# The second latent expert layer and the attention projections in plain float32, with half of that layer's gates carried by VectorE's one-hot operand

## The chip, the cores and the metric

One core of a Trainium2 chip runs the whole program in one launch. The metric is the device time of that launch in microseconds (us). Engines are named as in the profile: PE (TensorE matmul), PEld (its weight loads), DVE (VectorE), ACT (ScalarE), POOL (GpSimd), SP (SyncE, which issues most loads).

## The reference, cut to what matters

The model is a two-layer block with sparse attention, followed by a second block: per layer a mixer (gated delta rule in layer 0, grouped-query attention in layer 1) and an expert layer `peer` with 16384 experts. Only layer 1 of the second block is touched. All tensors are float32; there are 256 latent tokens of width 1024.

```python
def attention_mixer(h_ctx, h_lat, w_in, qn_g, kn_g, w_out, cos, sin, need_ctx_out):
    p = h @ w_in                  # 256 x 1024 by 1024 x 1536: q (8 heads), k and v (2 heads) of 128
    q_l = apply_rope(rmsnorm(q_l, qn_g), cos, sin); k_l = apply_rope(rmsnorm(k_l, kn_g), cos, sin)
    o_l = gqa_attend(q_l, concat(k_c, k_l), concat(v_c, v_l))     # softmax attention
    return o_l.reshape(B, T, ATT_Q_W) @ w_out                     # 256 x 1024 by 1024 x 1024
...
def peer(h, w_query, sub_keys, u_tab, v_tab):                     # per token x
    qry = (xb @ w_query).reshape(P, PEER_HEADS, 2, PEER_HALF)
    s = jnp.einsum('phcd,hckd->phck', qry, sub_keys)
    top_s, top_i = lax.top_k(s, PEER_TOPK)                        # 16 of 128, twice per head
    ...
    best_s, pos = lax.top_k(cand_s, PEER_TOPK)                    # 16 of the 256 pairs
    gate = jax.nn.softmax(best_s, axis=-1)
    act = jax.nn.gelu(jnp.einsum('pd,phkd->phk', xb, u_tab[idx]), approximate=False)
    return jnp.einsum('phk,phkd->pd', gate * act, v_tab[idx])
```

## The kernel before, in words

**The expert layer.** For the latent tokens `lat_peer` evaluates all 16384 experts densely: 128 chunks of 128 experts. `Dense.up` (L1876) multiplies one chunk's u-rows, two tiles `ut` of 128x512, with the normalised hidden state and puts gelu of it into the table G. `Dense.spread` (L1914) makes the gates of four tokens at a time: `L` holds a one-hot row of the second expert index times the gate (ACT: Abs, then Relu, L1923 and L1925), `R` a one-hot row of the first (DVE, L1926), and four matmuls `gp` multiply them. The gates are multiplied into G (L1938 where gelu is there already; else ACT copies them, L1940, and `up` multiplies later, L1910). `Dense.down` (L1956) multiplies G with the v-rows, one tile `vt` of 128x512 for each chunk and half of the output columns, 256 tiles in all.

**Layer 1 of it** keeps the first 48 tokens out of the dense work (`nb = 48`, so T = 208 columns): the class `Few` fetches their 16 experts per head by indirect DMA from POOL, 48 gathers for u-rows (`fg`, L1799, dotted on DVE at L1813) and 48 for v-rows (`gv`, L1737, summed on DVE at L1742). Each gather moves 128 rows of 4 KB; two buffers hold them (GB = 2).

**Precision.** A product is either plain float32 or *split*. `split` (L503) has ACT copy a weight tile rounded to fp32r (`sh`, L511) and DVE subtract (`sl`, L513); the activations are split once (`xs`). The product then is sh times [hi, lo], 416 or 512 columns, plus sl times hi. In layer 1 with `nb` the two halves land side by side in the bank and are added afterwards: in `up` by an ACT copy (L1902) and a DVE add (L1903). In `up` half of the contraction is split (four of eight steps), in `down` three of four chunks (`FD = 4`), there with a split of G as well (`gs`, L1976 and L1977). In the attention all of both projections is split (`lin_rows_split`, L537). In traces a plain float32 product appears as two MATMUL records, a split one as one record for each operand.

**Order.** A scheduler places the instructions; it runs on a model of its own. `weave(M.prep, ups, *WP)` mixes the routing (`peer_route`: 16 query projections `acs`, then top-k on DVE) with the first N0 = 56 chunks of `up`. `up_spread` then makes one spread for each of 52 chunks and does the last 20 alone. `down` follows, output half 0 then 1. Gathers are paced: `tick` adds its microseconds times a rate (FRATE = 0.1), and at each whole step one gather is traced under `issue_after(E.pin)`, where `E.pin` is the last instruction that was pinned (`split`'s subtraction, L513). They start at chunk 48 (`FAT`).

**Buffers.** Weight tiles come from one pool of five (UB = 5) tiles of 256 KB; a tile is free for its next load when its last reader is done: a split tile after ACT and DVE have read it, a plain tile after its last matmul. The banks `y` in PSUM (four) serve `up` and then `down`; `cf` has two buffers.

```python
UB, HB, VB, OB, N0, GB = 5, 5, 5, 2, 56, 2
DPS = dict(acc=1, ps=1, gp=2, y=4)
NB, FRATE, FAT, LAST = (0, 48), 0.1, 48, 48
```

Of the kernel before, what the change touches and what calls it, by code (L numbers as in the profile page):

```python
# [516 lines left out]
def split_x(E, P, hT, name, xs=None, nb=0):  # L517

    nc = E.nc
# [3 lines left out]
    for k in range(n):  # L523
        hi = xs[:, k, 0:256]
        if k % 2:
            nc.vector.tensor_copy(hi, hT[:, k])
# [3 lines left out]
        for lo, t in ((256, slice(nb, 256)), (512 - nb, slice(0, nb))):  # L530
            if t.stop > t.start:
                eng.tensor_tensor(out=xs[:, k, lo:lo + t.stop - t.start], in0=hT[:, k, t], in1=hi[:, t].bitcast(F32),
                                  op=ALU.subtract)
    return xs


def lin_rows_split(E, P, xs, w, width, fn):  # L537

    p = [acc(E) for _ in range(2)]
    for k in range(len(w)):  # L540
        h, l = split(E, P, w[k], k)
        for tt in range(2):
            for q, (o, wp) in enumerate(((0, h), (0, l), (256, h))):
                mm(E, p[tt][:, :width], xs[:, k, o + tt * 128:o + tt * 128 + 128], wp[:, :width], k == 0 and q == 0,
                   k == len(w) - 1 and q == 2)
    for tt in range(2):
        fn(tt, p[tt][:, :width])
# [9 lines left out]
def lin_cols_split(E, P, xs, ap, off, nt, fn, tag="acc", nb=0, xf=None):  # L557
# [4 lines left out]
    k0 = 4 if xf is not None else 0  # L562
    for t in range(nt):
        p = bank(E, tag, "acs")
        ws = wtile(E, ap, off + t * D * 128, 2, 512)
        for o in range(k0, 8, 4):
            h, l = split(E, P, ws[o // 4], o // 4)
            for k in range(4):
                c = slice(k * 128, k * 128 + 128)
# [1 line left out]
                end = o + k == 7 and not k0
                if nb:
                    mm(E, p, h[:, c], x, o + k == k0, False)
                    mm(E, p[:, 0:256], l[:, c], x[:, 0:256], False, end)
                else:
                    mm3(E, p[:, 0:256], h[:, c], l[:, c], x[:, 0:256], x[:, 256:512], o + k == k0, end)
# [3 lines left out]
        if nb:  # L580
            s = P.tile([128, 256], F32, name="ssum", tag="s", bufs=2)
            nc.scalar.copy(s[:, nb:256], p[:, 256:512 - nb])
            nc.scalar.copy(s[:, 0:nb], p[:, 512 - nb:512])
            nc.vector.tensor_tensor(out=s, in0=p[:, 0:256], in1=s, op=ALU.add)
            fn(t, s)
        else:
            fn(t, p[:, 0:256])
# [1252 lines left out]
class Dense:  # L1840
# [35 lines left out]
    def up(self, c, PU, n):  # L1876
# [10 lines left out]
        h, l = split(E, PU, us[0], 0)  # L1887
        for k in range(4):
            e = slice(k * 128, k * 128 + 128)
            x = self.xs[:, k, self.nb:self.nb + o1]  # L1890
            if self.nb:
                mm(E, p[:, 0:o1], h[:, e], x, k == 0, False)
                mm(E, p[:, 0:T], l[:, e], x[:, 0:T], False, False)
            else:
                mm3(E, p[:, 0:T], h[:, e], l[:, e], x[:, 0:T], x[:, T:o1], k == 0, False)
# [518 lines left out]
```

## Time and profile before

| what | value |
|---|---|
| runs (three) | 4258.22, 4268.22, 4280.0 us; median 4268.22 |
| profiled execution | 4277.75 us, span 4276.0 us, mean granted clock 0.942 |
| layer 1 of the second block in the span | attention from about 3225 us, routing from 3372, chunks from 3430, `down` from 3889 to 4264 us |
| PE, DVE, ACT, POOL busy in the whole span | 89%, 64%, 42%, 23% |

The profile is of one execution; times in it are counted from the start of its span. Matmuls overlap and their ends are modelled, so what one costs is read from the distance between starts in a dense stretch. The rest of the program, about 3225 us, is the same in both kernels.

### The profile page before, as it was taken

The page shows a single profiled execution, that of the slowest core. Times are in us where ns is not written, and L with a number is a line of the kernel's source. Part 1 is how long each engine was busy: PE and PEld are TensorE (multiplying, and loading weights), DVE is VectorE, ACT ScalarE, POOL GpSimd, SP SyncE. Part 2 cuts the span into 40 slices and gives each one's busy share as a digit, 9 for nine tenths or more (in the row PEclk, how much of TensorE's full clock was granted, in tenths as well). Part 3 has the DMA queues.
Part 4 walks back from the last instruction along what each step waited for, and adds up shares of the span by engine and source line. Part 5 has one row for each costly group of instructions (what it writes and reads, how often), then busy time and mean ns, then how long its engine had stood idle before and what let it go on. Part 6 is the DMA issues. An engine that isn't in the chain of part 4 may idle for free.

```text
span 4276.0 us, 66249 instructions
## 1 busy us (share of the span) xinstructions
PE 3790.3 (89%) x23253; PEld 3016.9 (71%) x23253; DVE 2721.5 (64%) x6361; ACT 1805.1 (42%) x4811; POOL 999.2 (23%) x973
## 2 busy tenths in 40 slices
PE   8787888979998799787789999999987899889998
PEld 6654565548555486674458899987866788888897
DVE  4683268568555684667328667766666696777764
ACT  3223212534225343422223379744434345984443
POOL 1010015453344532101002211112223122112110
PEclk8888998989998899898899999999999999999999
DMA  5443536899987996336334676688773256668875
GB/s 182 121 155 105 177 129 211 270 326 357 330 308 248 325 356 244 120 113 197 137 116 141 211 232 214 204 260 261 244 239 121 71 168 201 218 205 275 276 257 165
DMA packets 383518, 907.27 MB, mean 212 GB/s; under 512 B 87361, under 2 KB 89377, under 8 KB 382417
## 3 DMA queue, kind: packets, MB, share of 16 engines
q1 hardware_dynamic: 270080, 553.04, 39.0%
q0 software_dynamic: 87552, 318.81, 22.1%
q10 hardware_dynamic: 25552, 31.19, 2.4%
q8 instruction: 184, 3.01, 0.3%
q14 instruction: 150, 1.22, 0.1%
HBM read 887.56 MB, written 15.32 MB: 211 GB/s over the span
## 4 chain that ended last, share of the span: by engine, by line
PE 34%; DMA 15%; DVE 11%; ACT 5%; issue 4%; POOL 2%; SPq 0%; ACTq 0%; DVEq 0%; POOLq 0%
PE acc L392 8%; PE au L392 8%; PE y L392 7%; DMA vt<-in_peer_v_dram 7%; DMA ut<-in_peer_ut_dram 4%; PE acs L392 4%; DVE sl L513 3%; ACT sh L511 2%; PE gp L392 2%; DMA gv<-in_peer_v_dram,ixz 1%; DMA w<-in_ada_w_dram 1%; DMA w<-in_peer_wq_dram 1%; POOL cand L1659 1%; PE S L392 1%; PE o L392 1%
## 5 line engine op out<-in xcount | busy, mean ns | idle before, releaser
L392 PE MATMUL y<-gs,sh 128*128 128x512 f32 (+1 forms) x1536 | 540.8, 406 | 48.5 <-DVE gs L1977 43.9
L392 PE MATMUL au<-hp,ut 128*128 128x256 f32 (+1 forms) x2048 | 456.6, 366 | 0.3 <-issue 0.2
L513 DVE TENSOR_TENSOR sl<-vt,sh 128x512 fp32r<-128x512 f32 x384 | 268.2, 703 | 236.1 <-ACT sh L511 215.4
L392 PE MATMUL acc<-hdn,w 128*128 128x256 f32 x1536 | 378.4, 401 | 39.6 <-issue 17.0
L511 ACT CAST sh<-vt 128x512 fp32r<-128x512 f32 x384 | 236.8, 619 | 415.6 <-DMA vt<-in_peer_v_dram 359.2
L392 PE MATMUL y<-gs,sl 128*128 128x256 f32 (+1 forms) x1536 | 403.0, 273 | 5.0 <-DVE sl L513 4.9
L392 PE MATMUL au<-xs,sh 128*128 128x256 f32 (+1 forms) x1536 | 390.8, 334 | 18.0 <-DVE cf L1903 16.5
L392 PEld LDWEIGHTS au<-hp,ut 128*128 128x128 f32 x2048 | 365.7, 194 | 21.8 <-DMA ut<-in_peer_ut_dram 0.8
L1724 DVE SCALAR_TENSOR_TENSOR gu<-gu,h 128x1024 f32<-128x1024 f32 x256 | 311.6, 1223 | 90.4 <-DMA gu<-in_peer_u_dram,ixs 81.8
L392 PEld LDWEIGHTS acc<-hdn,w 128*128 128x128 f32 x1536 | 298.4, 200 | 97.0 <-issue 26.2
L392 PEld LDWEIGHTS y<-gs,sh 128*128 128x128 f32 x1536 | 292.2, 192 | 100.9 <-DVE gs L1977 61.1
L1722 POOL DMA_INDIRECT gu<-in_peer_u_dram,ixs x256 | 270.6, 1057 | 357.2 <-DVE gu L1724 223.6
L392 PE MATMUL au<-xs,sl 128*128 128x256 f32 (+1 forms) x1024 | 287.0, 280 | 22.3 <-DVE sl L513 21.8
L392 PEld LDWEIGHTS y<-gs,sl 128*128 128x128 f32 x1536 | 291.0, 193 | 14.8 <-DVE sl L513 9.2
L513 DVE TENSOR_TENSOR sl<-ut,sh 128x512 fp32r<-128x512 f32 x256 | 180.2, 705 | 168.9 <-ACT sh L511 161.6
L392 PEld LDWEIGHTS au<-xs,sh 128*128 128x128 f32 x1536 | 263.6, 193 | 30.3 <-DVE cf L1903 20.8
L1737 POOL DMA_INDIRECT gv<-in_peer_v_dram,ixz x128 | 138.5, 1082 | 613.7 <-DVE y L1742 573.2
L511 ACT CAST sh<-ut 128x512 fp32r<-128x512 f32 x256 | 159.9, 625 | 247.5 <-DMA ut<-in_peer_ut_dram 234.5
L392 PE MATMUL y<-G,vt 128*128 128x256 f32 (+1 forms) x1024 | 224.9, 362 | 0.0
L392 PEld LDWEIGHTS au<-xs,sl 128*128 128x128 f32 x1024 | 199.1, 194 | 28.0 <-DVE sl L513 27.7
L392 PE MATMUL acs<-xs,sh 128*128 128x256 f32 (+1 forms) x896 | 203.7, 318 | 8.7 <-ACT sh L511 4.9
L1925 ACT ACTIVATE ohl<-ohl,sl 128x128 f32<-128x128 f32 x464 | 207.3, 506 | 0.0
(637 smaller groups left out, 8009.6 us busy)
## 6 DMA issues: line engine op xcount, KB each, us to landing
ut<-in_peer_ut_dram SPq DMA_DIRECT2D x512, 256.0 KB
vt<-in_peer_v_dram SPq DMA_DIRECT2D x512, 256.0 KB
w<-in_ada_w_dram SPq DMA_DIRECT2D x96, 512.0 KB
w<-in_dn_w_in_dram SPq DMA_DIRECT2D x96, 512.0 KB
w<-in_w_up_dram SPq DMA_DIRECT2D x88, 512.0 KB
wd<-in_w_down_dram SPq DMA_DIRECT2D x44, 512.0 KB
w<-in_w_in_dram SPq DMA_DIRECT2D x40, 512.0 KB
w<-in_dn_w_out_dram SPq DMA_DIRECT2D x32, 512.0 KB
```

The costliest lines, as they stand in the source:

```text
L392: return E.nc.tensor.matmul(out, lhsT=lhsT, rhs=rhs, start=start, stop=stop)
L511: nc.scalar.copy(h, src)
L513: E.pin = eng.tensor_tensor(out=l, in0=src, in1=h.bitcast(F32), op=ALU.subtract).ins
L1659: nc.gpsimd.tensor_tensor(out=eq[:, h], in0=eq[:, h], in1=fi[:, h, None, :].to_broadcast([128, 16, 16]), op=ALU.mult)
L1722: nc.gpsimd.indirect_dma_start(out=g, out_offset=None, in_=E.a["peer_u"], in_offset=bass.IndirectOffsetOnAxis(ap=ix[:, s, k:k + 1], axis=0))
L1724: nc.vector.scalar_tensor_tensor(out=g, in0=g, scalar=1.0, in1=h, op0=ALU.mult, op1=ALU.mult, accum_out=c[:, k:k + 1])
L1737: nc.gpsimd.indirect_dma_start(out=g, out_offset=None, in_=E.a["peer_v"], in_offset=bass.IndirectOffsetOnAxis(ap=ix[:, k:k + 1], axis=0))
L1925: nc.scalar.activation(L[:, j], L[:, j], AF.Relu, scale=col(3, j), bias=col(2, j))
```

## The change

In layer 1 of the expert layer (`self.plain`, set where `xs` is None, which is where `nb` is not 0) every product is plain float32: `split_x`, all `split` calls, the `cf` sum, `gs` and the `ssum` of the query projections go. In `spread` two of the four tokens keep their gate in `L`; for the other two `L` is a bare one-hot (one Relu over both with constants) and the gate is multiplied into `R` by two DVE operations. `E.pin` is now set in `spread`, so after the last spread nothing new is pinned. The attention's projections use `lin_rows` on the plain hidden state. Layer 0 keeps its form.

```diff
@@ lin_cols_split
-    k0 = 4 if xf is not None else 0
+    k0 = 8 if xs is None else 4 if xf is not None else 0
...
         for k in range(k0):
-            mm(E, p[:, 0:256], ws[0][:, k * 128:k * 128 + 128], xf[:, k], False, k == k0 - 1)
+            w = ws[k // 4][:, k % 4 * 128:k % 4 * 128 + 128]
+            mm(E, p[:, 0:256], w, xf[:, k], k0 == 8 and k == 0, k == k0 - 1)
...
@@ Dense.up
+        if self.plain:
+            for k in range(4):
+                mm(E, p[:, 0:T], us[0][:, k * 128:k * 128 + 128], self.xf[:, 4 + k, nb:256], k == 0, False)
+        else:
...
-        if self.nb:
-            nc.scalar.copy(cf, p[:, T:o1])
-            nc.vector.tensor_tensor(out=cf, in0=p[:, 0:T], in1=cf, op=ALU.add)
...
-            nc.scalar.activation(cf[:, 0:n], y[:, 0:n], AF.Gelu)
+            cf = PU.tile([128, T], F32, name="cf", tag="cf", bufs=2)
+            nc.scalar.activation(cf[:, 0:n], p[:, 0:n], AF.Gelu)
@@ Dense.spread
-        for j in range(4):
+        a = 2 if self.plain else 4
+        for j in range(a):
             nc.scalar.activation(L[:, j], L[:, j], AF.Relu, scale=col(3, j), bias=col(2, j))
...
+        if a < 4:
+            nc.scalar.activation(L[:, a:4], L[:, a:4], AF.Relu, bias=1.0, scale=-1.0)
+        i = nc.vector.tensor_tensor(out=R[:, 0:a], in0=self.iota[:, None, :].to_broadcast([128, a, 128]),
+                                    in1=self.sl[:, 0, t:t + a, None].to_broadcast([128, a, 128]), op=ALU.is_equal).ins
+        if self.plain:
+            E.pin = i
+        for j in range(a, 4):
+            nc.vector.tensor_scalar(R[:, j], self.iota, col(0, j), col(2, j), op0=ALU.is_equal, op1=ALU.mult)
@@ Dense.down
-            if c % FD == FD - 1:
+            if self.plain or c % FD == FD - 1:
                 for k in range(4):
-                    mm(E, self.y[k][:, 0:T], vt[:, k * 128:k * 128 + 128], g, False, end)
+                    mm(E, self.y[k][:, 0:T], vt[:, k * 128:k * 128 + 128], g, first and c == cs[0], end)
                 continue
@@ attention
-            split_x(E, P, hT, "xs", xs)
...
-            lin_rows_split(E, PU, xs, w, 512, lambda tt, q: p.append(q))
+            lin_rows(E, hT, w, 512, lambda tt, q: p.append(q))
...
-            nc.scalar.copy(os[:, h, 0:256], o)
-            nc.vector.tensor_tensor(out=os[:, h, 256:512], in0=o, in1=os[:, h, 0:256].bitcast(F32), op=ALU.subtract)
+            evac(E, os[:, h], o)
...
-            lin_rows_split(E, PU, os, w, 512, fo)
+            lin_rows(E, os, w, 512, fo)
```

**Where the order moves.** PE near the end of `down`'s output half 0 in layer 1 (one order row of a plain product stands for one matmul call; `G1_29303` is the second half of the table G, `y_...` are the four banks, `yT` the turn of the finished sums). Before, the end of a group of four chunks, three split and one plain:

```order
L392 MATMUL y_33271<-gs_35179,sh_35182 128x416
L392 MATMUL y_33271<-gs_35179,sl_35183 128x208
L392 MATMUL y_33272<-gs_35179,sh_35182 128x416
L392 MATMUL y_33272<-gs_35179,sl_35183 128x208
L392 MATMUL y_33269<-G1_29303,vt_35194 128x208
L392 MATMUL y_33270<-G1_29303,vt_35194 128x208
L392 MATMUL y_33271<-G1_29303,vt_35194 128x208
L392 MATMUL y_33272<-G1_29303,vt_35194 128x208
L1999 MATMUL yT_35210<-cst0_58,ys_35200 128x128
```

Of the change, from the last spread through the last 21 chunks of `up` and the whole of half 0 (`G_27450` and `G_28473` are the two halves of G):

```order
L392 MATMUL gp<-ohr,ohl 128x128 x4
L392 MATMUL au<-hp,ut 128x208 x168
L392 MATMUL y<-G_27450,vt 128x208 x256
L392 MATMUL y<-G_28473,vt 128x208 x256
L1978 MATMUL yT<-cst_58,ys 128x128 x2
```

PE's operands in `up`'s tail and in `down` are now the loaded tiles and G themselves; no row between them reads what ACT or DVE made of a weight tile.

DVE in the last 20 chunks of `up`, after the last spread (the first row is that spread's own). `sl` is the low part of a weight tile, `cf` the gelu of a chunk, `fg` a gathered row block. Before:

```order
L1938 TENSOR_TENSOR G1_29303<-gp_32676,G1_29303 128x4x43
L513 TENSOR_TENSOR sl_32884<-ut_32879,sh_32883 128x512
L1910 TENSOR_TENSOR G1_29303<-G1_29303,cf_32705 128x208
L1910 TENSOR_TENSOR G1_29303<-G1_29303,cf_32734 128x208
L1903 TENSOR_TENSOR cf_32760<-au_32739,cf_32760 128x208
L1903 TENSOR_TENSOR cf_32789<-au_32765,cf_32789 128x208
L1910 TENSOR_TENSOR G1_29303<-G1_29303,cf_32760 128x208
L1910 TENSOR_TENSOR G1_29303<-G1_29303,cf_32789 128x208
L1903 TENSOR_TENSOR cf_32815<-au_32794,cf_32815 128x208
L1903 TENSOR_TENSOR cf_32844<-au_32820,cf_32844 128x208
L513 TENSOR_TENSOR sl_32910<-ut_32905,sh_32909 128x512
L1813 SCALAR_TENSOR_TENSOR fg_32925,fc_27859<-fg_32925,fh_32510 128x1024
```

Of the change, in the middle of the same 20 chunks (`fc` holds the dots of the gathered rows, `gv` is a block of gathered v-rows, `fy0_31447` the first of the three sums of them):

```order
L1879 TENSOR_TENSOR G1_28473<-G1_28473,cf_31137 128x208
L1786 SCALAR_TENSOR_TENSOR fg_31391,fc_27441<-fg_31391,fh_30854 128x1024
L1879 TENSOR_TENSOR G1_28473<-G1_28473,cf_31156 128x208
L1786 SCALAR_TENSOR_TENSOR fg_31418,fc_27441<-fg_31418,fh_30854 128x1024
L1790 TENSOR_TENSOR fc_27441<-fc_27441,fg_27440 128x48
L1879 TENSOR_TENSOR G1_28473<-G1_28473,cf_31172 128x208
L1713 TENSOR_SCALAR fy0_31447<-gv_31448,fc_27441 128x1024
L1879 TENSOR_TENSOR G1_28473<-G1_28473,cf_31191 128x208
L1715 SCALAR_TENSOR_TENSOR fy0_31447<-gv_31475,fc_27441,fy0_31447 128x1024
L1879 TENSOR_TENSOR G1_28473<-G1_28473,cf_31207 128x208
L1715 SCALAR_TENSOR_TENSOR fy0_31447<-gv_31502,fc_27441,fy0_31447 128x1024
```

The operations on gathers moved forward: between the multiplication of chunk 107 (the first of 208 columns, there are 21) and that of chunk 125 stand 18 of them, one for nearly every chunk; before, one stood for about every two and a half chunks, and the rest lay in `down`.

## Rows read from the trace of the kernel before

**Rows 1.** The page of the kernel before: PE's busy time, share and instructions, and the chain that ended last by engine.

```profile
PE 3790.3 (89%) x23253; PEld 3016.9 (71%) x23253; DVE 2721.5 (64%) x6361; ACT 1805.1 (42%) x4811; POOL 999.2 (23%) x973
PE 34%; DMA 15%; DVE 11%; ACT 5%; issue 4%; POOL 2%; SPq 0%; ACTq 0%; DVEq 0%; POOLq 0%
```

**Rows 2.** Busy time by stage: window, its length, then busy us (and instructions) of PE, PEld, DVE, ACT and POOL, granted clock, DMA share, GB/s. In order: attention and norm; query projections; 108 chunks with 52 spreads; a dense part of these; the last 20 chunks; `down` in two stretches; and 235 us of layer 0's spreads.

```profile
3225.00:3372.00 147.00, 114.76 (x523) 90.90 (x521) 105.94 (x196) 57.57 (x149) 53.08 (x46) 0.91 0.28 95
3372.00:3430.00 58.00, 56.52 (x303) 48.77 (x304) 37.79 (x172) 18.92 (x56) 3.20 (x5) 1.00 0.45 141
3430.00:3842.00 412.00, 371.85 (x2233) 355.60 (x2231) 305.45 (x807) 294.63 (x872) 80.31 (x84) 0.96 0.62 197
3640.00:3840.00 200.00, 177.00 (x1105) 168.09 (x1104) 146.16 (x328) 185.59 (x587) 27.43 (x29) 0.97 0.64 205
3842.00:3889.00 47.00, 43.14 (x258) 41.49 (x257) 32.41 (x75) 21.22 (x57) 7.93 (x9) 1.00 0.83 268
3889.00:4070.00 181.00, 165.78 (x1000) 158.71 (x1000) 130.12 (x228) 84.54 (x193) 37.52 (x33) 0.98 0.85 277
4070.00:4264.00 194.00, 180.11 (x1116) 173.28 (x1114) 114.47 (x221) 83.69 (x198) 18.25 (x16) 0.98 0.67 213
2510.00:2745.00 235.00, 235.00 (x1625) 222.93 (x1624) 184.63 (x324) 225.39 (x709) 34.92 (x37) 1.00 0.67 212
```

**Rows 3.** Timeline of PE in the last chunks of layer 1's `up`: start us, us, engine, line, operation, count. One whole chunk, from its first split matmul to the first of the next.

```profile
3847.90 0.50 PE L392 MATMUL au<-xs,sh 128*128 128x416 f32 x1
...
3848.64 0.37 PE L392 MATMUL au<-xs,sh 128*128 128x416 f32 x1
...
3848.94 0.36 PE L392 MATMUL au<-xs,sh 128*128 128x416 f32 x1
...
3850.51 0.50 PE L392 MATMUL au<-xs,sh 128*128 128x416 f32 x1
```

**Rows 4.** Timeline of PE in layer 0's spreads: the plain half of one chunk (4 products of 256 columns, 8 records), its four gate products, and the plain half of the next chunk.

```profile
2581.64 1.89 PE L392 MATMUL au<-hp,ut 128*128 128x256 f32 x8
2583.37 1.05 PE L392 MATMUL gp<-ohr,ohl 128*128 128x128 f32 x8
2584.18 0.48 PE L392 MATMUL au<-xs,sh 128*128 128x256 f32 x2
...
2585.70 1.89 PE L392 MATMUL au<-hp,ut 128*128 128x256 f32 x8
```

**Rows 5.** Groups of ACT instructions from 3640 to 3840 us: line, operation, shapes, count, busy us, mean ns, idle before.

```profile
L1925 ACT ACTIVATE ohl<-ohl,sl 128x128 f32<-128x128 f32 x179 | 77.3, 491 | 0.0
L511 ACT CAST sh<-ut 128x512 fp32r<-128x512 f32 x48 | 29.8, 621 | 11.5 <-DMA ut<-in_peer_ut_dram 11.5
L1902 ACT COPY cf<-au 128x208 f32<-128x208 f32 x45 | 15.3, 342 | 0.0
```

**Rows 6.** The same for DVE.

```profile
L1813 DVE SCALAR_TENSOR_TENSOR fg<-fg,fh 128x1024 f32<-128x1024 f32 x29 | 35.3, 1218 | 2.3 <-DMA fh<-hl_d 2.3
L513 DVE TENSOR_TENSOR sl<-ut,sh 128x512 fp32r<-128x512 f32 x47 | 32.4, 688 | 13.7 <-ACT sh L511 13.6
L1926 DVE TENSOR_TENSOR ohr<-iota,sl 128x512 f32<-128x512 f32 x44 | 30.1, 685 | 0.0
L1903 DVE TENSOR_TENSOR cf<-au,cf 128x208 f32<-128x208 f32 x46 | 16.9, 370 | 1.6 <-ACT cf L1902 1.6
```

**Rows 7.** Timeline of POOL near the end of layer 0's `down`, where nothing paces the gathers: the first and the last of six in a row.

```profile
3126.73 0.94 POOL L1737 DMA_INDIRECT gv<-in_peer_v_dram,ixz  x1 [1.21 <-DVE y L1742]
...
3146.51 0.94 POOL L1737 DMA_INDIRECT gv<-in_peer_v_dram,ixz  x1 [2.25 <-DVE y L1742]
```

**Rows 8.** Waits from 3889 to 4264 us: engine and line, what it waited for, us in total, times, longest.

```profile
ACT sh L511 <- DMA vt<-in_peer_v_dram: 170.9, 98, 4.4
PEld y L392 <- DVE gs L1977: 35.6, 40, 3.6
```

**Rows 9.** The chain that ended last, in order of time, in `down`: start us, us, what. Loads of weight tiles.

```profile
3893.48 4.51 DMA vt<-in_peer_v_dram
3899.38 3.65 DMA vt<-in_peer_v_dram
3904.43 5.16 DMA vt<-in_peer_v_dram
...
4025.98 7.08 DMA vt<-in_peer_v_dram
```

**Rows 10.** Busy time of the dots on gathered u-rows (L1813) in the last 20 chunks; each gather counts twice, as the product and as the read of its sum.

```profile
3842.00:3889.00 47.00, 8.95 (x16) 1.00 0.83 268
```

**Rows 11.** Timeline of PE: two waits in the attention's first projection, the first and the last of the 96 split matmuls of its second, and the starts of two query projections.

```profile
3250.77 0.80 PE L392 MATMUL acc<-sh,xs 128*128 128x512 f32 x1 [3.44 <-DVE xs L526]
3281.01 0.69 PE L2146 MATMUL ps<-cst,hry 128*128 128x128 f32 x4 [3.30 <-DVE hry L2138]
3336.04 0.58 PE L392 MATMUL acc<-sh,xs 128*128 128x512 f32 x1
...
3358.79 0.39 PE L392 MATMUL acc<-sh,xs 128*128 128x512 f32 x1
...
3375.18 0.58 PE L392 MATMUL acs<-xs,sh 128*128 128x512 f32 x1
...
3378.30 0.58 PE L392 MATMUL acs<-xs,sh 128*128 128x512 f32 x1
```

More of the change, by code (lines that the diff above doesn't have):

```diff
@@ L514, in split, with split_x @@
     return h, l
-def split_x(E, P, hT, name, xs=None, nb=0):
+def split_x(E, P, hT, name, xs=None):
     nc = E.nc
@@ L529, in split_x @@
         eng = nc.vector if k % 2 else nc.gpsimd
[L530 to L533, printed above, removed]
-    return xs
[L537 to L547, printed above, removed]
+        eng.tensor_tensor(out=xs[:, k, 256:512], in0=hT[:, k], in1=hi.bitcast(F32), op=ALU.subtract)
+    return xs
 def mm3(E, o, h, l, xh, xl, start, stop):
@@ L570, in lin_cols_split @@
                 x = xs[:, o - k0 + k]
[L571 to L576, printed above, removed]
+                mm3(E, p[:, 0:256], h[:, c], l[:, c], x[:, 0:256], x[:, 256:512], o + k == k0, o + k == 7 and not k0)
         for k in range(k0):
-            mm(E, p[:, 0:256], ws[0][:, k * 128:k * 128 + 128], xf[:, k], False, k == k0 - 1)
+            w = ws[k // 4][:, k % 4 * 128:k % 4 * 128 + 128]
+            mm(E, p[:, 0:256], w, xf[:, k], k0 == 8 and k == 0, k == k0 - 1)
         tick(E, 2.7)
[L580 to L587, printed above, removed]
+        fn(t, p[:, 0:256])
 def softmax_pairs(E, pool, jobs, causal, scale):
@@ L1847, in __init__ @@
         self.xf, self.xs = x
+        self.plain = self.xs is None
         self.nb = few.nb if few else 0
@@ L1886, in up @@
             us.append(ut)
[L1887 to L1890, printed above, removed]
-            if self.nb:
[L1892 to L1895, printed above, removed]
+        if self.plain:
+            for k in range(4):
+                mm(E, p[:, 0:T], us[0][:, k * 128:k * 128 + 128], self.xf[:, 4 + k, nb:256], k == 0, False)
+        else:
+            h, l = split(E, PU, us[0], 0)
+            for k in range(4):
+                e = slice(k * 128, k * 128 + 128)
+                x = self.xs[:, k]
+                mm3(E, p[:, 0:T], h[:, e], l[:, e], x[:, 0:T], x[:, 256:512], k == 0, False)
         for k in range(4):
@@ L2184, in attention @@
     with tc.tile_pool(name="atp", bufs=1) as P, tc.tile_pool(name="atw", bufs=2) as WK, \
-            tc.tile_pool(name="ats", bufs=4) as PU:
-        xs = P.tile([128, 8, 512], F32R, name="xs")
+            tc.tile_pool(name="ath", bufs=1) as PH:
         kT = P.tile([128, 2, 256], F32, name="kTl")
@@ L2189, in attention @@
         qT = P.tile([128, 8, 256], F32, name="qT")
-        with tc.tile_pool(name="ath", bufs=1) as PH:
-            hT = norm_T(E, PH, xl, A, "hat", shift=B)
-            split_x(E, P, hT, "xs", xs)
+        hT = norm_T(E, PH, xl, A, "hat", shift=B)
         def rows(n, nh, gcs, dst):
@@ L2206, in attention @@
             rows(n, 4, E.qg, qT[:, n * 4:n * 4 + 4])
-        os = P.tile([128, 8, 512], F32R, name="xs")
+        os = PH.tile([128, 8, 256], F32, name="hat", tag="hT")
         sc = 128.0 ** -0.5
```

21 lines of the change are left out of this document (9 added, 12 removed).

## The prediction

> **What bounds the kernel now.** I begin with the page [rows 1]. PE is busy for 89% of the span, yet the chain that ended last lies on PE for 34% only and on DMA for 15%: stages with different limits take turns. So I read the stages by windows [rows 2], in the stretch after 3225 us alone, where the change lies. The reader is to see there which engine is full in each stage. From 3640 to 3840 us, spreads beside chunks, ACT is busy for 185.6 of 200 us, PE for 177 and DVE for 146: ACT sets the pace. The stretch holds 47 spreads (about 179 Relu's in four [rows 5], some records missing), so a chunk with its spread takes 200/47 = 4.26 us. In the last 20 chunks no engine is full, but PE comes first with 43 of 47 us. In `down` PE is busy for 346 of 375 us and the DMA share is 0.85, then 0.67; the waits name the loads of `vt`, which hold ACT for 170.9 us, and behind them the split of G and of the tile, which holds PE for 35.6 us [rows 8].
>
> **Prices of a product.** A split product of 208 columns: one chunk of `up` goes from 3847.90 to 3850.51, 2.61 us, and two split records of 416 columns stand 0.30 us apart with the one of 208 between them [rows 3]. A plain product: 8 records of 256 columns take 2583.37 - 2581.64 = 1.73 us [rows 4], 0.216 each, so 0.176 for 208 columns and 0.351 for a product of two records. That checks: 4 x 0.30 + 4 x 0.351 = 2.60. Four gate products: 2584.18 - 2583.37 = 0.81. So plain costs PE 17% more than split, and frees ACT and DVE. The Trainium skill, page "FP8 and Floating Point Precision", section "TensorE Precision Notes", speaks against the change more strongly: true FP32 there is four passes (the high and low halves each with each), which against the three of a split product would make 0.40 of the 0.30, not 0.351. The rows decide here, with 1.17 for 1.33.
>
> **The change part by part**, against the profiled execution of 4277.75 us (span 4276.0, some 2 us around it; it is 9.5 us above the median of 4268.22). All that is done before 3225 us is the same, so I count it at nothing.
>
> *Attention.* 96 split records of 512 columns take 3358.79 - 3336.04 us and one more, 0.239 each [rows 11]; a product of three is 0.72, a plain one 512/208 x 0.351 = 0.864. The 80 products (5 weight blocks of 8 steps and 2 token tiles) gain 80 x 0.146 = +11.7 us on PE. Two waits of PE, 3.44 us for `xs` and 3.30 us for `hry` [rows 11], end with subtractions that the change removes (the second one's maker stood on POOL behind them): -6.7. Sum +5; ends -3 (more of this stage's waits go; PE is busy for 115 of its 147 us [rows 2]) and +12 (the waits stay).
>
> *Query projections.* From 3.12 us each [rows 11] to 8 x 256/208 x 0.351 = 3.46: 16 x 0.34 = +5.4, with ends +4 and +7. The `ssum` that goes was off PE.
>
> *Chunks and spreads.* A chunk is now 8 x 0.351 = 2.81 us of PE. For each chunk with a spread, ACT loses the cast (0.62), the copy of `cf` (0.34) and one Relu (two become one of double width, about 0.4) [rows 5], and falls from about 3.95 busy us to about 2.6 to 3.1; DVE loses the subtraction (0.69) and the add (0.37), and the one-hot goes from 0.685 to about 0.42 for half the width plus two gate operations of 128 columns, which I put at 0.28 each (smaller than any row here; between nothing and 0.37) [rows 6], so it falls from 3.1 to about 2.4. PE has 2.81 + 0.81 = 3.63 and becomes the bound. Layer 0 shows such a stage: PE busy for all of 235 us with ACT at 225 [rows 2], and a chunk of 1.73 + 0.81 + split half in 2585.70 - 2581.64 = 4.06 us, with no gap [rows 4]. So 56 x 2.81 + 52 x 3.63 = 346 us. Before, 56 x 2.61 + 52 x 4.26 = 368 of the 412 us; 44 were stalls. PE's waits on the low part of a tile go, and of the stalls I keep 12 (from 2 to 31). 412 to 358: -54, ends -64 and -35.
>
> *The last 20 chunks.* Before, 47 us for 20 x 2.61 = 52 less the first ones that had run ahead. PE alone would now take 20 x 2.81 = 56. But what paces the gathers is gone: after the last spread `E.pin` is stale, and the order puts 18 operations on gathered rows between the multiplications of chunks 107 and 125 on DVE. Before, 8 dots lay there (16 records [rows 10]). A multiplication stands behind a gather's operation on DVE, gelu needs one of two `cf`, PE needs the bank that gelu reads: so PE waits for gathers. With two buffers and nothing to pace them a gather takes (3146.51 - 3126.73)/5 = 3.96 us [rows 7]; 18 x 3.96 = 71 us. 47 to 71: +24. Ends: +9 (PE alone), +37 (a gather 0.7 us slower, as the loads of `ut` run at share 0.83 beside them [rows 2]).
>
> *`down`.* 256 tiles x 4 x 0.351 = 359.7 us of PE. No split of G or of tiles stands between load and matmul, so the 35.6 us go; but a plain tile is held until its matmuls end. A slot's turn is the landing plus 0.1 (a load followed 1.40 us after a landing where cast and subtraction take 1.31 [rows 5, 6, 9]) plus 1.405; five slots keep up with PE while landing is under 5 x 1.405 - 1.5 = 5.5 us. Most landings on the chain are, 3.65 and 5.16 for instance; some are not, 7.08 [rows 9]. I add 3 us at the start and 9 us for late loads: 372 for 375, -3; ends -13 (nothing late) and +20 (a late load of 1 us for every 11 tiles or so). The gathers left, 39 of 48 v-rows, need 39 x 3.96 = 154 us, within `down`. What follows `down` I leave as it is.
>
> *Sum:* +5 +5.4 -54 +24 -3 = -22.6. Profiled execution 4255; as a difference to the median 4268.22, **4246 us**. The ends taken as independent (root of their squares) give about 27 on either side.
>
> **The rivals.** *R1, PE alone decides:* the gathers' operations arrive early enough, as the chunks start with several loads ahead: tail 56, `down` 363. That is 15 and 9 less: 4222. For it: PE had 1.00 in layer 0's spreads [rows 2]. Against: 18 operations in a fixed order on DVE.
>
> *R2, unpaced gathers take the DMA engines from `vt`:* a gather moves 524 KB in 3.96 us, 132 GB/s [rows 7]. Of the 277 GB/s that the first half of `down` moved [rows 2], 145 are left, 262 KB / 145 = 1.81 us for each tile during 154 us, 85 tiles x 0.40 = +34, less the 9 already in: 4271, no change. For it: PE asks for 187 GB/s, and 187 + 132 is 319, where 277 took share 0.85 (326 at 1). Against: it is still below. The Trainium skill, page "DMA: Bandwidth & Descriptors", section "SWDGE vs HWDGE vs iDMA", has the two kinds of queue served in turn inside each DMA engine, which would make gathers cost loads their turn as R2 says; no run here shows it yet.
>
> *R3, slots bind, and it is slower:* in `down` and in the first 56 chunks (368 tiles) plain tiles held to the end of their matmuls leave the loads too late. It decides from a mean landing of 5.5 us; the gain is eaten at about 5.95, since (0.086 x 368) is 32. Midway between 5.5 and the longest, 7.08, at 6.3: (6.3 + 1.5)/5 = 1.56 a tile, +0.155 x 368 = +57, less 9: 4294. Against: in `up`'s spread stage DMA share is 0.64, and landings near 4 to 5 are the rule.
>
> *R4, a plain product is dearer than in layer 0:* with its four products of halves for the three of a split one, 4/3 of 0.30 is 0.40 in place of 0.351; 8 of them in 128 chunks (0.39 each) and 4 in 256 tiles (0.195) are +100 us: 4346. That is the time by the page of the Trainium skill named above. The rows of plain products nearly exclude it.
>
> That the change doesn't do what it says is no rival with a time: the order shows plain operands throughout `up` and `down`.
>
> **How the numbers follow.** Forecast 0.47, R1 0.20, R2 0.22, R3 0.10, R4 0.01. A measurement of this kernel can tell about 0.5%, 21 us, from no change, so faster is below 4247, which cuts the forecast in half: of its 0.47, 0.24 is faster, 0.21 the same, 0.02 slower. R1 is faster, R2 the same but for 0.02, R3 slower but for 0.02. Faster 0.44, same 0.43, slower 0.13. The forecast's own range is 4219 to 4273. The whole range, 4214 to 4282, holds nine tenths of it, three quarters of R1, most of R2 and the mild part of R3: 0.79.
>
> **What would show it.** In the spread stage: 3.63 us from spread to spread, PE near 100%, ACT under 80%. After the last spread: 71 us for 20 chunks, PE waiting on `cf` or a bank behind DVE's gather operations; at 56 us R1 is right. In `down`: 1.405 us from tile to tile and PE's waits on `vt` 12 us in all; with waits while gathers run and none after the last, R2; with waits throughout and landings over 5.5 us, R3. Query projections 3.46 us apart, attention 152 us. The forecast is wrong if a plain chunk alone takes other than 2.81 us, or if ACT or DVE is full in the spreads.

## The result, and the profile of the changed kernel

The changed kernel takes 4240.52 us (median of 10 runs, 4224.85 to 4252.92), the kernel before 4266.98 us (10 runs); the ratio is 0.9934, with a 95% interval of 0.9919 to 0.9948, that is 28 us less (22 to 35). Forecast was 4246 (range 4214 to 4282). The profiled executions differ by more than the medians: 4277.75 and 4244.35 us, spans 4276.0 and 4242.3. Of these 33.7 us, 3.5 are there already where the change begins, in work that is the same in both.

For stages I use marks that both traces have: the start of the last turn `yT` of layer 0's output, of the first softmax matmul `S`, of the last `o`, of the first query projection `acs`, of the first `au`, of the first and the last `gp`, of the last `au`, of the last `yT`.

| stage, from mark to mark | before | changed | difference | forecast |
|---|---|---|---|---|
| `yT` to `S`: norm, first projection | 59.4 | 50.8 | -8.6 | |
| `S` to last `o`: softmax part | 49.7 | 42.5 | -7.2 | |
| last `o` to `acs`: second projection, norm | 36.2 | 39.4 | +3.2 | |
| these three: attention | 145.3 | 132.7 | -12.6 | +5 |
| query projections | 58.0 | 61.7 | +3.7 | +5.4 |
| `up` to the last spread | 409.0 | 360.4 | -48.6 | -54 |
| tail of `up` | 46.8 | 68.6 | +21.8 | +24 |
| `down` | 379.0 | 384.5 | +5.5 | -3 |
| to the end | 11.0 | 11.0 | 0 | 0 |
| sum | 1049.1 | 1018.9 | -30.2 | -22.6 |

Each column is one trace. Stages with the same code differ between traces by up to some 6 us: the attention of before reads 141.4 to 145.3 us (here, e2, e5, e8), `down` of before 379.0 to 383.4 (here, e1, e5, e10, e12), the changed `down` 384.0 to 389.8 (here, e2, e3, e4). A difference of that size in one stage is not to be leaned on.

The page of the changed kernel, to be read against [rows 1]: busy time by engine, and the chain that ended last.

```profile
PE 3825.8 (90%) x23173; PEld 3050.0 (72%) x23173; DVE 2383.5 (56%) x5727; ACT 1488.9 (35%) x4041; POOL 949.4 (22%) x945
PE 41%; DMA 11%; DVE 9%; issue 4%; ACT 2%; POOL 2%; SPq 0%; ACTq 0%; DVEq 0%; POOLq 0%
```

PE works 35.5 us more in a program that is 34 us shorter; ACT is relieved of 316 us, DVE of 338. More of the chain lies on PE, 41% for 34%. By stage, with the columns of [rows 2]: norm, first projection, softmax part, query projections, `up` before the first spread, `up` with spreads, its tail, and two stretches of `down`.

```profile
3222.20:3230.40 8.20, 4.64 (x35) 3.53 (x33) 5.29 (x12) 4.63 (x9) 0.70 (x1) 1.00 0.87 303
3230.40:3274.20 43.80, 43.80 (x119) 20.32 (x120) 11.07 (x22) 10.10 (x42) 10.62 (x12) 1.00 0.56 189
3274.20:3316.70 42.50, 38.85 (x200) 32.47 (x199) 29.62 (x83) 21.25 (x55) 4.27 (x3) 0.96 0.07 26
...
3356.10:3417.80 61.70, 61.34 (x308) 54.54 (x309) 33.28 (x187) 7.78 (x15) 3.96 (x7) 1.00 0.47 146
3417.80:3574.70 156.90, 151.49 (x852) 149.22 (x851) 75.52 (x276) 29.81 (x77) 36.08 (x44) 0.99 0.59 178
3574.70:3778.20 203.50, 201.74 (x1297) 200.90 (x1296) 136.33 (x365) 153.88 (x515) 34.87 (x37) 1.00 0.77 242
3778.20:3846.80 68.60, 63.72 (x339) 61.27 (x339) 28.74 (x51) 7.04 (x24) 17.07 (x18) 0.95 0.87 299
3846.80:4040.00 193.20, 184.48 (x1018) 179.25 (x1017) 52.33 (x45) 0.69 (x2) 36.84 (x40) 0.99 0.84 282
4040.00:4231.30 191.30, 191.30 (x1106) 190.77 (x1104) 3.12 (x5) 2.98 (x8) 0.26 (x1) 0.99 0.56 173
```

The kernel before between the same marks, norm, first projection, softmax part, and the stage with spreads:

```profile
3225.70:3238.10 12.40, 5.31 (x36) 4.08 (x34) 8.76 (x15) 5.85 (x12) 3.64 (x3) 0.82 0.90 341
3238.10:3286.30 48.20, 39.27 (x157) 29.86 (x156) 38.17 (x54) 17.35 (x51) 29.38 (x25) 0.90 0.54 176
3286.30:3335.10 48.80, 39.83 (x207) 33.71 (x206) 34.68 (x91) 24.16 (x68) 7.75 (x6) 0.93 0.01 4
...
3557.80:3839.20 281.40, 254.62 (x1571) 243.27 (x1569) 189.94 (x417) 235.72 (x732) 39.85 (x40) 0.97 0.67 213
```

The reader is to see that PE is busy for 201.74 of 203.5 us with spreads, with ACT at 76% (93% in the dense part before, more than PE [rows 2]), and that it is busy without a gap, at full clock, in the first projection, where it had been idle for 9 of 48 us. The lengths of the two stages with spreads, 281.4 and 203.5 us, are not to be subtracted: by the `au` records, 16 to a chunk, 39 chunks stood before the first spread, 72 in the stage with spreads and 17 behind it; in the changed kernel these are 52, 55 and 21, around the same 52 spreads.

The pieces beneath are in the changed kernel's timeline of PE (as [rows 3, 4]): from one set of gate products to the next with one chunk between them, then a dense piece of `down`, and what else PE does there.

```profile
3681.08 1.05 PE L392 MATMUL gp<-ohr,ohl 128*128 128x128 f32 x8
3681.97 2.98 PE L392 MATMUL au<-hp,ut 128*128 128x208 f32 x16
3684.79 1.05 PE L392 MATMUL gp<-ohr,ohl 128*128 128x128 f32 x8
...
4099.82 101.44 PE L392 MATMUL y<-G,vt 128*128 128x208 f32 x576
4201.10 4.31 PE L392 MATMUL yf<-cst,fy 128*128 128x16 f32 x38
```

A chunk with a spread takes 3.71 us (forecast 3.63), the chunk alone 3684.79 - 3681.97 = 2.82 (2.81); 576 records of `down`, 72 tiles, take 4201.10 - 4099.82 = 101.28 us, 1.407 a tile (1.405).

### The profile page after: what moved, and what is told of

It is laid out like the page before. It is cut to its first block, busy times and chain, and to the rows that moved or that the text cites. A ratio compares the mean times of both kernels' runs of the same rounds, so it can differ in the third digit from the quotient of the medians.

```text
span 4242.3 us, 63981 instructions
## 1 busy us (share of the span) xinstructions
PE 3825.8 (90%) x23173; PEld 3050.0 (72%) x23173; DVE 2383.5 (56%) x5727; ACT 1488.9 (35%) x4041; POOL 949.4 (22%) x945
## 4 chain that ended last, share of the span: by engine, by line
PE 41%; DMA 11%; DVE 9%; issue 4%; ACT 2%; POOL 2%; SPq 0%; ACTq 0%; DVEq 0%; POOLq 0%
PE y L392 12%; PE au L392 9%; PE acc L392 8%; PE acs L392 4%; DMA vt<-in_peer_v_dram 4%; PE gp L392 2%; DMA gv<-in_peer_v_dram,ixz 2%; DMA ut<-in_peer_ut_dram 2%; DVE sl L513 1%; DMA w<-in_ada_w_dram 1%; POOL cand L1632 1%; DMA w<-in_peer_wq_dram 1%; DVE tmp L1367 1%; PE o L392 1%; PE S L392 1%
## 5 line engine op out<-in xcount | busy, mean ns | idle before, releaser
L392 PE MATMUL au<-hp,ut 128*128 128x208 f32 (+1 forms) x3072 | 620.0, 355 | 8.5 <-ACT cf L1878 4.3
L392 PEld LDWEIGHTS au<-hp,ut 128*128 128x128 f32 x3072 | 546.0, 191 | 32.9 <-issue 5.4
L392 PE MATMUL y<-G,vt 128*128 128x208 f32 (+1 forms) x2560 | 492.4, 350 | 8.7 <-DMA vt<-in_peer_v_dram 5.2
L392 PEld LDWEIGHTS y<-G,vt 128*128 128x128 f32 x2560 | 455.6, 192 | 27.2 <-DMA vt<-in_peer_v_dram 9.3
L392 PE MATMUL acc<-hdn,w 128*128 128x256 f32 x1536 | 375.0, 398 | 42.5 <-issue 17.7
L392 PE MATMUL y<-gs,sh 128*128 128x512 f32 x768 | 284.5, 422 | 20.1 <-DVE gs L1953 17.2
L392 PE MATMUL y<-gs,sl 128*128 128x256 f32 x768 | 204.3, 284 | 6.9 <-DVE sl L513 6.7
L392 PE MATMUL au<-xs,sh 128*128 128x256 f32 x1024 | 207.2, 299 | 0.6 <-ACT sh L511 0.5
L392 PE MATMUL acs<-xs,sh 128*128 128x256 f32 x832 | 179.1, 312 | 6.1 <-ACT sh L511 4.4
L1715 DVE SCALAR_TENSOR_TENSOR y<-gv,col,y 128x1024 f32<-128x1024 f32 x127 | 164.5, 1296 | 33.7 <-DMA gv<-in_peer_v_dram,ixz 33.6
L392 PE MATMUL acs<-hff,w 128*128 128x256 f32 x704 | 168.2, 380 | 0.0
```

The source lines that it names most:

```text
L392: return E.nc.tensor.matmul(out, lhsT=lhsT, rhs=rhs, start=start, stop=stop)
L1715: nc.vector.scalar_tensor_tensor(out=y, in0=g, scalar=c[:, k:k + 1], in1=y, op0=ALU.mult, op1=ALU.add)
```

## The experiments

Each ratio is to the kernel before, with its 95% interval; in us of 4268. The changed kernel has 0.9934, -28.

**e1 and e2: the two halves.** e1 is the kernel before with the changed attention; e2 the changed kernel with the attention of before. Of e1's edit, the two calls (the operand of the second, and the pools, which go with them, are left out):

```diff
...
-            lin_rows_split(E, PU, xs, w, 512, lambda tt, q: p.append(q))
+            lin_rows(E, hT, w, 512, lambda tt, q: p.append(q))
...
-            lin_rows_split(E, PU, os, w, 512, fo)
+            lin_rows(E, os, w, 512, fo)
```

> The kernel before, with the attention's projections alone in plain float32. Theory: the two traces show the attention 11 us shorter (norm -4.2, first projection -4.4, softmax part -6.3, second projection +3.8), since ACT, DVE and POOL no longer stand in front of PE there; so about 11 us less than before (4256). Rival, as the prediction had it: PE pays more for plain products than the waits give back, +5 us (4272).

Measured: 4251.65 us, 0.9969 (0.9954 to 0.9983), -13.

> The changed kernel with the attention's projections split as before. Theory: the expert layer alone is worth -28 + 11 = -17 us against before (4250), its stages reading -3 (norm), +5 (query projections), -49 (chunks with spreads), +22 (tail), +5 (down). Rival, the prediction's +5 for the attention: -33 us (4234).

Measured: 4246.05 us, 0.9958 (0.9939 to 0.9976), -18. The halves add up (-31 for -28). The attention is a gain; the +5 of the prediction is outside e1's interval (-20 to -7).

**e10 and e12: which projection.** e10 has only the second of the two lines above (with its operand), e12 only the first.

> The kernel before with the attention's second projection alone in plain float32 (with its operand os unsplit). Theory: the softmax part loses 7 us, since ACT's casts of w_out and the split of os stood before the softmax on ACT and DVE; the second projection costs PE 4.7 more; first projection unchanged: -2.5 us (4261). Rival: the softmax part gains from the first projection's earlier end: +5 us (4269).

Measured: 4264.88 us, 0.9985 (0.9971 to 1.0), -6 (-12 to 0). In its trace the softmax part falls only from 49.7 to 47.8, not by 7, and the second projection rises from 22.8 to 27.2, as forecast; from `yT` to `S` it reads 56.4 for 59.4, though nothing is changed there. The part of the theory on the softmax is wrong; its sum is within the interval. The rival's +5 is outside it.

> The kernel before with the attention's first projection alone in plain float32 (the second and its operand split as before). Theory: it is the first projection that carries the attention's gain, through PE's gaps and the low clock that follows each: the stretch to the first softmax matmul falls from 59 to about 51 us, and the softmax part, where a gap of 5.5 us and some 7 us of low clock go as well, from 50 to about 43; second projection unchanged: 14 us less than before (4252). Rival: the softmax part is held by the casts of w_out, which are still there, and stays at 48 or more: 8 us less (4258).

Measured: 4251.14 us, 0.9954 (0.9939 to 0.9968), -20 (-26 to -13). From `yT` to `S` 50.7 us, the softmax part 41.4, the second projection 22.5. So the first projection carries the whole of the attention's gain; the plain second one costs PE some 4.5 us. How, the granted clock shows. The kernel before, in stretches of 4 us (PE's busy time, clock, DMA share, GB/s):

```profile
3230.90:3234.90 4.00, 0.00 (x0) 0.84 1.01 400
3234.90:3238.90 4.00, 2.63 (x10) 0.50 1.02 411
3238.90:3242.90 4.00, 4.00 (x18) 0.80 1.05 404
3246.90:3250.90 4.00, 0.56 (x3) 0.98 0.41 159
3250.90:3254.90 4.00, 4.00 (x11) 0.60 0.65 201
3282.90:3286.90 4.00, 4.00 (x17) 0.76 0.53 179
3294.90:3298.90 4.00, 0.38 (x1) 0.52 0.01 2
3298.90:3302.90 4.00, 4.00 (x15) 0.62 0.00 0
```

The changed kernel, through its first projection, and at the longest gap after it:

```profile
3231.40:3271.40 40.00, 40.00 (x105) 1.00 0.54 183
3279.40:3283.40 4.00, 3.58 (x11) 0.62 0.00 0
```

The gaps, in PE's timeline of the kernel before:

```profile
3235.83 1.08 PE L453 MATMUL ps<-cst,hatxn 128*128 128x128 f32 x4 [5.15 <-ACT hatxn L444]
...
3298.52 1.22 PE L392 MATMUL S<-kTc,qT 128*128 128x256 f32 x2 [5.46 <-ACT ap L2234]
```

and the same two of the changed kernel:

```profile
3228.75 0.63 PE L453 MATMUL ps<-cst,hatxn 128*128 128x128 f32 x4 [1.53 <-DVE hatxn L446]
...
3279.82 0.71 PE L392 MATMUL S<-kTc,qT 128*128 128x256 f32 x2 [2.01 <-ACT ap L2210]
```

The other two long gaps of the kernel before, 3.44 us at 3250.77 and 3.30 at 3281.01, stand in [rows 11]. Behind each of the four the slices read a lowered granted clock, 0.50, 0.60, 0.76 and 0.62 of full speed (the lower of the two levels is 0.5; a slice between the levels holds both). In the changed kernel the gap of 1.53 us is followed by 1.00, and the gap of 2.01 us still by 0.62.

The 15.8 us from `yT` to the last `o` can be added up from these rows, as an estimate. PE's idle time (length less busy time of norm, first projection and softmax part) was 7.1 + 8.9 + 9.0 = 25.0 us and is 3.6 + 0 + 3.6 = 7.2: 17.8 less. The low clock, taken as the busy time of a slice times what its clock lacks of 1, cost 6.4 us in the slices shown and costs 1.4: 5.0 less. The 48 products of the first projection cost 48 x 0.146 = 7.0 more. That is 15.8.

**e4 and e5: half of the gates.** e4 is the changed kernel with all gates in ACT; e5 the kernel before with half of them in DVE's operand and nothing else.

```diff
-        a = 2 if self.plain else 4
+        a = 4
```

> The changed kernel with all four gates of a spread in ACT's Relu as before (one DVE one-hot of full width). Theory: the casts that went were what filled ACT; it gets back 2 x 0.48 - 0.40 = 0.56 us a spread, 29 us on 154 of a stage of 203 us in which PE is full, so the stage grows by little, 3 us (0 to 12). Rival: ACT becomes the bound again and the half of the gates in DVE's operand carries the gain: +29 us (4270).

Measured: 4237.66 us, 0.9936 (0.9915 to 0.9957), -27. Its stage with spreads:

```profile
3575.20:3778.30 203.10, 201.87 (x1297) 201.05 (x1297) 123.79 (x265) 171.60 (x566) 34.20 (x37) 1.00 0.76 243
```

ACT gets 18 us of work back, less than the 29 worked out, and PE is as full as it was (the chunks before, among and behind the spreads are as many as in the changed kernel): beside plain products the halved gates are worth nothing that can be measured.

> The kernel before with the other half of the change alone: in layer 1 two of four gates go into DVE's operand, all products stay split. Theory: the stage of spreads is bound by ACT there (186 of 200 us); a spread takes 0.56 us less of ACT and 0.43 more of DVE, 52 x 0.56 = -29 us at most; I expect -20 (4245). Rival: ACT is full of work that PE does not wait for, and the stage is held by the chain cast, subtraction, matmul, copy, add through two busy engines; then -5 or nothing (4260 to 4265).

Measured: 4249.28 us, 0.9963 (0.9946 to 0.998), -16 (-23 to -9). Its stage with spreads:

```profile
3546.60:3803.60 257.00, 242.99 (x1553) 233.51 (x1552) 199.13 (x514) 212.51 (x680) 40.49 (x39) 0.99 0.71 231
```

281 has become 257, and ACT's work in it 212.51 us for 235.72, while DVE's has grown: ACT was the bound, and the rival is out. Either half of the change takes it off; together they gain hardly more than the plain products alone. Not all of the 24 us reaches the end: one chunk more stands behind the last spread, so the tail reads 50.3 for 46.9 us, and `down` reads 382.9 for 379.0.

**e3: the pacing of the tail.**

```diff
-            nc.vector.tensor_tensor(out=g[:, 0:n], in0=g[:, 0:n], in1=cf[:, 0:n], op=ALU.mult)
+            i = nc.vector.tensor_tensor(out=g[:, 0:n], in0=g[:, 0:n], in1=cf[:, 0:n], op=ALU.mult).ins
+            if self.plain and n == T:
+                E.pin = i
```

> The changed kernel with E.pin set as well by the multiplication of each of the last 20 chunks, so that gathers stay paced there: the order has 11 gather operations between those chunks on DVE in place of 20. Theory: gathers on DVE hold the tail; it falls from 68.6 to about 57 us, down holds ten gathers more but within its length, so 12 us less than the changed kernel (4228, 39 less than before). Rival: the tail waits for the loads of u-rows, not for gathers: tail stays at 66 to 69 us, no difference to the changed kernel (4240).

Measured: 4236.0 us, 0.9924 (0.9903 to 0.9944), -32: not to be told from the changed kernel. In the trace the tail is 61.9 us for 68.6, and `down` 386.3 for 384.5. What it mends is seen in the changed kernel's timelines. DVE: dots on gathered rows and what they waited for.

```profile
3803.17 1.23 DVE L1786 SCALAR_TENSOR_TENSOR fg<-fg,fh 128x1024 f32<-128x1024 f32 x1 [3.01 <-DMA fg<-in_peer_u_dram,fix]
...
3806.44 1.23 DVE L1786 SCALAR_TENSOR_TENSOR fg<-fg,fh 128x1024 f32<-128x1024 f32 x1 [1.75 <-DMA fg<-in_peer_u_dram,fix]
...
3810.61 1.23 DVE L1786 SCALAR_TENSOR_TENSOR fg<-fg,fh 128x1024 f32<-128x1024 f32 x1 [2.36 <-DMA fg<-in_peer_u_dram,fix]
...
3814.25 1.23 DVE L1786 SCALAR_TENSOR_TENSOR fg<-fg,fh 128x1024 f32<-128x1024 f32 x1 [2.12 <-DMA fg<-in_peer_u_dram,fix]
...
3818.82 1.23 DVE L1786 SCALAR_TENSOR_TENSOR fg<-fg,fh 128x1024 f32<-128x1024 f32 x1 [3.04 <-DMA fg<-in_peer_u_dram,fix]
```

PE in the same stretch, and ACT at the end of PE's wait:

```profile
3795.95 20.37 PE L392 MATMUL au<-hp,ut 128*128 128x208 f32 x112 [0.36 <-DMA ut<-in_peer_ut_dram]
3820.61 1.75 PE L392 MATMUL au<-hp,ut 128*128 128x208 f32 x4 [4.29 <-ACT cf L1878]
```

```profile
3820.08 0.24 ACT L1789 ACTIVATE fc<-fc 128x48 f32<-128x48 f32 x1 [11.40 <-DVE fg L1786]
```

The tail of e3, to be read against 3778.20:3846.80 above:

```profile
3788.20:3850.10 61.90, 60.09 (x338) 58.66 (x337) 21.35 (x45) 7.18 (x21) 9.60 (x11) 1.00 0.83 259
```

The dots come every 3.3 to 4.6 us, as gathers land ((3818.82 - 3803.17)/4 = 3.91), and PE, once the four banks are used up, stands for 4.29 us behind them. That wait came by way of ACT: it stood 11.40 us at L1789, the gelu of all the gathered dots, until the last of them was in, with the gelus of chunks behind it. In e3 PE is idle for 1.8 us in place of 4.9, and the granted clock reads 1.00 for 0.95, which makes some 3 us more. So the pacing is worth 7 us of the tail's 21.8 by these two traces, and 3 to 7 when the unpaced tails of e2 and e4, 66.0 and 65.0 us, are counted. The rest is its content: 21 chunks follow the last spread (168 plain calls, 8 to a chunk), before 17 (204 calls, 12 to a chunk). 21 x 2.81 is 59, 17 x 2.61 is 44.

**e6, e7 and e8: `down` and the weight tiles.** e6 is the changed kernel with three split tiles of four in `down`, as before; e7 the changed kernel with 8 weight tiles in layer 1's `up` and `down`, from a pool of their own; e8 the kernel before with 8 in its `down` alone. Of e6's edit (the sums of the split halves, which come back with it, are left out):

```diff
-            if self.plain or c % FD == FD - 1:
+            if c % FD == FD - 1:
...
```

e8's edit (e7 takes `ut` from the same pool too, which it opens before `up`):

```diff
-            vt = E.wp.tile([128, 512], F32, name="vt", tag="w")
+            vt = self.wp.tile([128, 512], F32, name="vt", tag="w")
...
+                PQ = tc.tile_pool(name=nm + "W", bufs=8, side="right")
+                M.wp = PQ.__enter__() if nb else E.wp
...
```

> The changed kernel with down split as before (three tiles of four). Theory: PE has only 328 us of work in down, but loads into five tiles bound it at the 379 us of before; the splits set E.pin again, so the tail is paced as in e3 (62 us): 5 + 6 = 11 us less than the changed kernel (4229). Rival: it was ACT and DVE, now free of the rest, or the pacing, that held down before, and it falls below 360: 25 to 45 us less (4195 to 4215).

Measured: 4228.57 us, 0.9915 (0.9897 to 0.9934), -36; tail 61.2 us, `down` 377.2. The size is as expected, and the rival (`down` below 360) is out, but its interval overlaps that of the changed kernel.

> The changed kernel with 8 weight tiles in place of 5 for layer 1's up and down. Theory (slots): PE's 9 us of waits on vt while gathers run go, so 9 us less (4231). Rival (DMA engines): they are busy for 0.91 of that stretch, more tiles only wait longer: no change (4240).

Measured: 4225.83 us, 0.9904 (0.9884 to 0.9923), -41; `down` 375.4 for 384.5, and the stretch with spreads has no gap of PE at all. The first half of `down`, in which the gathers run, in e7 (to be read against 3846.80:4040.00 above):

```profile
3843.10:4040.00 196.90, 195.02 (x1103) 194.31 (x1102) 54.02 (x47) 2.18 (x6) 36.88 (x40) 0.99 0.85 290
```

In the changed kernel PE was idle there for 8.7 us: 3.4 at the start, behind the gelus of the last chunks, and 5.3 behind loads of `vt` (the idle times of its timeline; PEld's own waits come to 9.3). Its waits, and two of the loads on the chain that ended last:

```profile
PEld y L392 <- DMA vt<-in_peer_v_dram: 9.3, 13, 1.2
```

```profile
3869.56 5.75 DMA vt<-in_peer_v_dram
...
3881.28 6.47 DMA vt<-in_peer_v_dram
```

Each such load begins when a matmul has freed its tile. All these waits fall into the time of the gathers: the last ends at 4002.07, the last gather is issued at 3995.31. With 8 tiles there is none, and gathers and loads run side by side at 290 GB/s: the waits were for tiles, not for a rate that the DMA engines lack.

> The kernel before with 8 weight tiles in place of 5 in layer 1's down. Theory: a load lands 4 to 6 us after its tile is free and five tiles give one per (landing + 1.4)/5 = 1.1 to 1.5 us, against 1.25 of PE; with 8 the loads run ahead and down falls from 379 towards PE's 328 us: 30 us less (4235). Rival: down waits for the split of G and of the tile on ACT and DVE or for the DMA engines at share 0.85, no change (4265).

Measured: 4224.1 us, 0.9904 (0.9883 to 0.9925), -41: more than the 30 expected; three more tiles in the kernel before are worth at least as much as the whole change (-28; the intervals just overlap). Its `down`, from mark to mark, and that of e6:

```profile
3865.30:4205.80 340.50, 332.88 (x2122) 329.19 (x2120) 245.69 (x453) 173.08 (x396) 71.07 (x50) 0.99 0.81 275
```

```profile
3829.40:4206.60 377.20, 345.29 (x2121) 329.59 (x2121) 245.86 (x451) 169.28 (x394) 57.06 (x50) 0.99 0.74 244
```

And ACT's waits there for loads of `vt`, e8 first (to be read against [rows 8]: 170.9 us):

```profile
ACT sh L511 <- DMA vt<-in_peer_v_dram: 29.9, 26, 3.4
```

```profile
ACT sh L511 <- DMA vt<-in_peer_v_dram: 170.1, 100, 3.9
```

With 8 tiles ACT waits 30 us in place of 170, and the DMA engines move 275 GB/s, not 244: they had not been the limit.

**e9 and e11: put together.** e9 is the changed kernel with e6's and e7's edits; e11 the kernel before with e1's, e5's and e8's, so that `up` and the query projections stay split.

> The changed kernel with down split as before and 8 weight tiles in layer 1's up and down. Theory: the gains add: down 384 to 340 (as in the kernel before with 8 tiles), tail 69 to 61, the rest of up -2; with the changed kernel's 28 about 82 us less than before (4183). Rival: split down and the loads of v-rows want ACT, DVE and DMA engines that in this kernel the 39 later gathers use: down stays at 360 or more, 60 us less than before (4205).

Measured: 4176.9 us, 0.9773 (0.9758 to 0.9789), -97. The stage with spreads, the tail and `down` of e9:

```profile
3576.70:3766.50 189.80, 189.80 (x1232) 189.80 (x1231) 132.69 (x359) 152.31 (x511) 31.70 (x34) 1.00 0.76 241
3766.50:3826.30 59.80, 59.24 (x338) 58.92 (x337) 18.81 (x41) 7.23 (x24) 8.79 (x9) 1.00 0.84 273
3826.30:4160.30 334.00, 331.34 (x2123) 328.52 (x2121) 244.49 (x451) 172.26 (x394) 68.47 (x50) 0.99 0.82 274
```

PE is full in all three. It beats both kernels, by 2.3% the one before, and by 15 us more than the 82 worked out: `down` falls by 50.5 us, not 44, and the rest of the 15 is not placed. (In e7 and e9 the first spread comes four chunks later, so that their stage with spreads is shorter than the changed kernel's 203.5 us by its content; from the first chunk to the last spread it is 358.3 us for 360.4.) From e7 to e9 only the products of `down` change: with 8 tiles it takes 375.4 us with plain ones and 334.0 with split ones, and the tail, paced again by the splits, falls from 68.5 to 59.8.

> The kernel before with the gates halved (as e5), plain attention (as e1) and 8 weight tiles in down (as e8): up and query projections stay split. Theory: -16 -13 -40 = -69 us (4195), 13 more than e9, which is what plain products in up are worth beside halved gates. Rival: with casts gone from nowhere else ACT stays full in the spreads and the sum falls short, -50 (4214).

Measured: 4193.32 us, 0.9807 (0.9788 to 0.9827), -82. Its stage with spreads is 256.7 us, as in e5. e9 is 15 us faster by the ratios, near the 13 expected; the intervals just touch. That is not the price of plain products in `up` and the query projections alone, since e9 has its 8 tiles in `up` as well. By stages, e9 against e11: query projections +6 us, `up` with its tail 17 less, `down` 5 less.

## Why the prediction was right, and where not

The sum was right (-22.6 for -28 measured, -30.2 in the traces), in part by luck: the attention came out 17.6 us under its term, `down` and the chunks 8.5 and 5.4 us over theirs, and the tail had its size by another account than the one given.

- **Chunks and spreads**, the term that decides: right in its mechanism. PE becomes the bound, a chunk with spread takes 3.71 us, the stretch 360 us (358 forecast). But 107 chunks stand in it for 111 before, so some 10 of its 48.6 us are four chunks (4 x 2.61) that now stand in the tail; stretch and tail together are the fair test, -26.8 for -30. The 4.26 us rest on 47 spreads; the 179 Relus are 45 spreads, and 47 is the number of chunks, which takes some 4 us off the 44 of stalls and changes nothing else. The prices of plain products from layer 0 hold. That the halved gates are needed for it is not so (e4). The 0.40 of R4 is excluded: 1.407/4 is 0.352. The Trainium skill (page "FP8 and Floating Point Precision", section "TensorE Precision Notes") counts four passes for true FP32. By that count, as an estimate, a pass of a plain product costs 0.352/4 = 0.088 us, against 0.30/3 = 0.10 for one of the three products of a split one; so four against three was not the ratio of the prices here, which is 1.17.
- **Attention:** wrong in sign. The step failed that set the 6.7 us of two waits against 11.7 us on PE. The prediction left out the 5.15 us before the norm's turns and the 5.46 us before the softmax's, which go with the first projection's splits as well (e12, not e10), and that PE's clock is low for some us behind each gap. -12.6 in place of +5, outside the ends (-3 to +12). Of PE's price the prediction was right: the plain second projection costs 27.2 us for 22.8.
- **Query projections:** near, +3.7 for +5.4, just under the lower end of +4. All traces together give 61.1 to 62.2 us for plain and 55.3 to 58.0 for split ones, +3 to +7.
- **Tail:** right in size, by luck, on a wrong account. Gathers hold PE, as forecast, but for 3 to 7 us (e3), and in the longest wait by way of ACT; the base of "20 chunks, less the first ones that had run ahead" was 17 chunks before and is 21 now, so that 15 us are four chunks more, moved here from the stretch before, and the dearer product. With pacing 61.9 remain. R1's 56 was out of reach.
- **`down`:** +5.5 for -3, within the ends. The sum of 372 left out what PE does there besides tiles, `yf` and `yT`, some 7.8 us by their starts (5.2 of it `yf`), while the 375 held it. The start is the 3 us forecast (3.4); the late loads are 5.3 us for 9. With some 4 us at a granted clock of 0.99 that is 381; the last 4 us are not placed. R2's sign is there, at a small size: PE waits on `vt` while gathers run and not after the last, for 5.3 us and not 34. R2's reason is not: in e7 gathers and loads move as before, and three more tiles end the waits. The Trainium skill (page "DMA: Bandwidth & Descriptors", section "SWDGE vs HWDGE vs iDMA") has each DMA engine go round the queues in turn, those that GpSimd feeds and those that SyncE and ScalarE feed. The landings of 5.75 to 6.47 us beside gathers fit that, but no run here tells it from another way of sharing. R3's slots bind as well: those landings are above its 5.5 us, and five tiles turn them into the 5.3 us of waits. Far more they bind with split tiles: 379 us of the kernel before fall to 340 with 8 tiles (e8). I had read [rows 8] as a price of splitting that the change would save; it was mostly a price of five tiles, and the change paid it in PE work instead.

## What to carry to other kernels

When an engine off the critical path is full, take the cheapest work off it and look what becomes the bound: here the extra pass of PE and the halved gates relieved the same engine, and the second one was worth nothing. Before making PE's work dearer to get rid of waits behind loads, give the loads more buffers: three tiles more in `down` gave 41 us, plain products in `down` lost some 5 to 7 us with five tiles, and 41 with eight (e7 and e9). And look how the order moves work across the marks before two stages are compared. Count a gap of PE together with the low clock behind it.
